# Unused bytes at the ends of two SBUF pools: a diffusion block with hi/lo matmuls, before and after

## The chip, the core and the metric

The kernel runs on one NeuronCore of a Trainium2 chip. Five engines share an on-chip memory, SBUF, of 128 partitions: TensorE (PE in the rows; PEld is its loading of stationary operands), VectorE (DVE), ScalarE (ACT), GpSimd (POOL) and SyncE (SP), which here issues nearly all DMAs. The metric is the device time of one execution in microseconds.

## The reference, cut to what matters

One layer of a diffusion block over 1024 latent tokens of width 1024, with 256 context tokens that are needed only for the end states of a recurrence:

```python
h_c = modulate(rms_norm(ctx, norm1_w), csh1, csc1)
parts_c = split(h_c @ w_in[:, :4096])               # q, forget fwd, forget bwd, i
o_c, s_f, s_b = hgrn_bidir(*parts_c, ..., zero_state, zero_state)
h_x = modulate(rms_norm(x, norm1_w), sh1, sc1)
parts_x = split(h_x @ w_in)                         # 9 parts of 1024 columns
o_x, _, _ = hgrn_bidir(*parts_x[:4], ..., s_f, s_b)
y_a = sgu(gelu(u), gelu(v), ...)                    # spatial gating unit
y_b = hgrn_readout(o_x, og, hgrn_norm_w)
y = (sigmoid(gate_a) * (y_a @ w_a) + sigmoid(gate_b) * (y_b @ w_b)) @ w_o
x = x + g1 * y
h2 = modulate(rms_norm(x, norm2_w), sh2, sc2)
a, v = split(h2 @ w_up)                             # 2 x 2816 columns
x = x + g2 * ((gelu(dwconv_grid(a)) * v) @ w_down)
return rms_norm(x, final_norm_w)
```

## The kernel before, in words

All float32 products of large matrices are made of three matmuls. `mm3` (lines 83 to 89) takes two operands that are each split into a rounded part and a rest, of type float32r, and adds hi x hi (line 87), hi x lo (88) and lo x hi (89) into one PSUM bank; a bank holds 512 float32 and has the tag `pj` or `hg`. In a row `pj<-hxh,whi` the first name behind the arrow is the moving operand (256 or 512 columns) and the second the stationary one (128 columns, loaded anew for every matmul). `load_unit` fetches 512 KB of weights into `wraw` (three buffers), ScalarE makes `whi` of it (line 68), GpSimd or VectorE makes `wlo` (line 69).

The stages follow each other in the program: modulation vectors and context (to about 135 us), eight HGRN heads (to about 880), the gating unit with the `u` projection, gates and branches (880 to 1330), the output projection (to 1426), the ConvFFN's up projection with its convolution on VectorE (lines 1014 and 1016, to 1923), and the down projection (to the end). In most stages the activations move 512 columns at a time against stationary weights: `hxh`/`hxl` in the projections, `yah`/`yal` and `ybh`/`ybl` in the branches, `h2h`/`h2l` in the up projection. In the down projection it is the other way: 512 columns of `w_down` move, and a 128-token slice of `hh`/`hl` (a split hidden tile) is stationary. `hid_split` puts the hidden tiles 0 and 1 and, of each half's tail, the first two (`hs0p if i < 2 else dn`) into the pool `hs0p`; in the second half the tail tiles of the first half come first and are used again. So of 44 uses of a hidden tile (22 tiles, two halves) 8 are from `hs0p` and 36 from `dn`; a use is 8 token blocks x 3 matmuls. In the rows `hh` and `hl` stand for both pools.

The order of all work is the order of the code, with some writes of `tc.issue_after` for ScalarE and VectorE; nothing in it depends on addresses. Pools named "left" (`const`, `wp`, `h1`, `s0p`, `m1`, `ff`, `hs0p`) are stacked up from the low end of SBUF, those named "right" (`hc`, `tmp0`, `ctp`, `hp`, `r1`, `r2`, `sp`, `gp`, `h2`, `bcp`, `cv`, `dn`) down from the high end, and each tile takes its bytes per partition, rounded up to 32. So an address follows from the sizes of the pools that lie below (or above) it. These are the starts, in bytes within a partition; for a pool of several tiles the first:

| Buffers | Use on TensorE | Start before | mod 128 before | Start after | mod 128 after |
|---|---|---|---|---|---|
| `whi` / `wlo` | stationary; moving in the token-major projections, the context's `i`, output and down projections | 17280 / 29568 | 0 | +128 | 0 |
| `hxh`, `mh` | moving, or stationary against 256 columns | 41856 | 0 | 41984 | 0 |
| `hh`, `hl` in `hs0p` | stationary, 512 columns | 131968 | 0 | 132096 | 0 |
| `hh`, `hl` in `dn` | stationary, 512 columns | 184224 | 32 | 183744 | 64 |
| `h2h` / `h2l` | moving, 512 columns | 163808 / 196576 | 96 | 163328 / 196096 | 0 |
| `yah`, `ybh` / `yal`, `ybl` | moving, 512 columns | 131040 / 163808 | 96 | 130560 / 163328 | 0 |
| `hch` / `hcl` | moving or stationary, 256 columns | 212960 / 221152 | 96 | 212480 / 220672 | 0 |
| HGRN tiles `dm`, `e2`, `qb`, `ka`, `v`, `S`, `b` | both, plain float32, 128 columns or fewer | 118432 (`dm`) | 32 | 117952 | 64 |
| HGRN tiles `kt`, `asum`, `osb`; `vt` | stationary, plain float32 | 218976 (`kt`) | 96 | 218496 | 0 |
| `wst`; `vc` | moving, plain float32 | 116224; 116864 | 0 | 115744; 116384 | 32 |
| `apad0` / `apad1` | none (VectorE reads them) | 154272 / 159040 | 32 / 64 | 153792 / 158560 | 64 / 96 |

Slices that a matmul takes of these tiles lie whole multiples of 512 bytes behind the start.

Of the kernel before, what the change touches and what calls it, by code (L numbers as in the profile page):

```python
# [8 lines left out]
F32 = mybir.dt.float32  # L9
# [4 lines left out]
PSUM = bass.MemoryType.PSUM  # L14
DRAM = bass.MemoryType.DRAM

P = 128
# [18 lines left out]
def kernel(  # L36
# [16 lines left out]

    # ------------------------------------------------------------------ pools
    const, close_const = pool("const", "left")
# [16 lines left out]
    def load_unit(src, k0, nk, c0, ncol, lo_eng=None):  # L72
        """weights src[k0*128:(k0+nk)*128, c0:c0+ncol] as two float32r parts [p, k, col]"""
        raw = wp.tile([P, 1024], F32, tag="wraw", name="wraw", bufs=W_RAW)
        last_load[0] = nc.sync.dma_start(
            out=raw.rearrange("p (k n) -> p k n", n=ncol),
            in_=src[k0 * P:(k0 + nk) * P, c0:c0 + ncol].rearrange("(k p) n -> p k n", p=P),
        )
        hi, lo = split_unit(raw, lo_eng)
        v = lambda t: t.rearrange("p (k n) -> p k n", n=ncol)  # L80
        return v(hi), v(lo)

    def mm3(ps, a, b, first, last):
        """ps += a.T @ b for two-part operands a, b"""
        ah, al = a
        bh, bl = b
        nc.tensor.matmul(ps, lhsT=ah, rhs=bh, start=first, stop=False)  # L87
        nc.tensor.matmul(ps, lhsT=ah, rhs=bl, start=False, stop=False)  # L88
        nc.tensor.matmul(ps, lhsT=al, rhs=bh, start=False, stop=last)  # L89

    # -------------------------------------------------------------- constants
    ident = const.tile([P, P], F32, name="ident")
    make_identity(nc, ident)
    ones = const.tile([P, P], F32, name="ones")
# [4 lines left out]
    nc.vector.memset(scanm, 1.0)  # L99
    nc.vector.memset(scanm.rearrange("p (c t) -> p c t", t=CH)[:, :, 0:1], 0.0)  # L100
    hc, close_hc = pool("hc", "right")
    tmp0, close_tmp0 = pool("tmp0", "right")
    trif = tmp0.tile([P, P], F32, name="trif")
    # causal in the direction of the scan, scores transposed [s, t]: two blocks, two directions
    mask = const.tile([P, 2, 2, P], U8, name="mask")
    for d in range(2):
        nc.gpsimd.affine_select(
            out=trif, in_=ones, pattern=[[1 if d == 0 else -1, P]], base=0,
            channel_multiplier=-1 if d == 0 else 1, compare_op=ALU.is_ge, fill=0.0)
        for i in range(2):  # L110
            nc.vector.tensor_copy(out=mask[:, i, d, :], in_=trif)

    ins_of = lambda r: getattr(r, "ins", r)

    def rsqrt(dst, src, n):
        nc.gpsimd.tensor_tensor(out=dst, in0=src, in1=mhalf[:, :n], op=ALU.pow)

    # PSUM: banks of 512 float32
    psp, close_psp = pool("psp", space=PSUM)
# [6 lines left out]

    # ---------------------------------------------------- parameters as columns
    rows = {}
# [28 lines left out]

    # lower bounds: softmax over the depth axis (length one), its cumulative sum less the first row
    lb = const.tile([P, 16], F32, name="lb")
# [13 lines left out]

    # -------------------------------------- modulation: shift1, scale1 (both streams)
    def norm_pair(xt, after):
        """the two row blocks xt[:, i, :] over their rms"""
        ss = const.tile([P, 2], F32, tag="ss", name="ss", bufs=2)
        rs = const.tile([P, 2], F32, tag="rs", name="rs", bufs=2)
        for i in range(2):
            junk = tmp0.tile([P, D], F32, tag="junk", name="junk", bufs=1)  # L180
            with tc.issue_after(after):
                nc.scalar.activation(out=junk, in_=xt[:, i, :], func=AF.Square, accum_out=ss[:, i:i + 1])
        with tc.issue_after(after):
            nc.vector.tensor_scalar(out=ss, in0=ss, scalar1=1.0 / D, scalar2=RMS_EPS, op0=ALU.mult, op1=ALU.add)
        rsqrt(rs, ss, 2)
        for i in range(2):
            with tc.issue_after(after):
                nc.vector.tensor_scalar(out=xt[:, i, :], in0=xt[:, i, :], scalar1=rs[:, i:i + 1], scalar2=None,
                                        op0=ALU.mult)

    ring = lambda: tmp0.tile([P, 2, D], F32, tag="ring", name="ring", bufs=4)
    ctp, close_ctp = pool("ctp", "right")
    # by the tensor engine; of columns 1536..2047 the vector engine sums the first row blocks
    sel = const.tile([P, 2, 2], F32, name="sel")
# [73 lines left out]

    # ------------------------------------------------------ context: final states
    WI = w_in[0]  # L270
# [27 lines left out]
    def first_half(t, d):  # L298
        """the half of each 128-block that comes first in direction d; t [p, blk, 2, 64]"""
        return t[:, :, d, :]  # L300
# [83 lines left out]

    # latent stream
    hxh = [h1.tile([P, T], F32R, name=f"hxh{k}") for k in range(KC)]
# [59 lines left out]

    # --------------------------------------------------------- latent: HGRN2 heads
    hp, close_hp = pool("hp", "right")
# [5 lines left out]

    # the first tags lie where the spatial gating unit starts, the last ones where the context ends
    lead = {}
# [17 lines left out]
    def firsts(t, off, step, nchunk):  # L474
        """[p, d, chunk, t]: of direction d (at off + d * step) the half of each chunk that d meets first"""
        a = t[:]
        return bass.AP(tensor=a.tensor, offset=a.offset + off,
                       ap=[list(a.ap[0]), [step + CH // 2, 2], [CH, nchunk], [1, CH // 2]])
# [3 lines left out]
    def project(off, h, dst_fn, lo_eng=None):  # L482
        """feature-major projection of 128 columns; dst_fn(seg, psum)"""
        wh, wl = load_unit(WI, 0, KC, off + h * P, P, lo_eng)
        for s in range(2):
            ps = pj()
            for k in range(KC):
                mm3(ps, (wh[:, k, :], wl[:, k, :]),
                    (hxh[k][:, s * 512:(s + 1) * 512], hxl[k][:, s * 512:(s + 1) * 512]), k == 0, k == KC - 1)
            dst_fn(s, ps)  # L490

    def token_major(units, n2):
        """token-major projection of two blocks, 256 columns"""
        ps = pj()
        for j in range(2):
            n = 2 * n2 + j
            for k in range(KC):
                wh, wl = units[k // 4]
                mm3(ps[:, j * 256:(j + 1) * 256],
                    (hxh[k][:, n * P:(n + 1) * P], hxl[k][:, n * P:(n + 1) * P]),  # L500
                    (wh[:, k % 4, :], wl[:, k % 4, :]), k == 0, k == KC - 1)
        return ps
# [18 lines left out]
    def finish(h, og, osbs):  # L521
        """read-out of a head, features on partitions, gated; to DRAM"""
        for s in range(2):
# [9 lines left out]
    for h in range(NH):  # L533
# [40 lines left out]
        def state(d, n):  # L574
            """state that block n of direction d starts from"""
            if (d == 0 and n == 0) or (d == 1 and n == NT - 1):
                return s0[:, h, d, :]
            return S[:, d, n, :]

        for st in range(2):  # L580
# [24 lines left out]
            for d in range(2):  # L605
# [17 lines left out]
                                        in1=elv[:, d, :, (1 - d):(2 - d)].to_broadcast([P, 4, CH]), op=ALU.mult)  # L623
            # scores, transposed: [s, t]; pairs with s after and t before the reference are never formed
            nc.scalar.copy(out=firsts(e2z, 0, 0, 8), in_=firsts(e2, 0, 512, 8))
# [63 lines left out]

    # ----------------------------------------------- spatial gating unit (branch A)  # L690
    r1, close_r1 = pool("r1", "right")
# [7 lines left out]
    for q in range(2):  # L699
# [3 lines left out]
        nc.vector.tensor_copy(out=wst[:, 4 * q:4 * q + 4, :].rearrange("p g t -> p (g t)"), in_=tp)  # L703
    # C[d, g, t] = ln_b[d] * sum_s w[g, t, s] + b[g, t]
    for q in range(2):
# [62 lines left out]

    # ---------------------------------------------------------- branches, merged
    gp, close_gp = pool("gp", "right")  # L770
    # modulation rows gate1, shift2, scale2, gate2 (latent): a step is 128 rows of ada_w
    mod_acc = {}
# [86 lines left out]

    # --------------------------------------------- output projection, residual, norm 2  # L860
    close_gp()
# [13 lines left out]
    bcast_row(b2b, mod_d[3])  # L875
    # the residual input, then the updated stream times its norm-2 gain
    xa = [bcp.tile([P, D], F32, name=f"xa{n}") for n in range(NT)]
# [78 lines left out]

    # ------------------------------------------------------------------- ConvFFN
    ff, close_ff = pool("ff", "left")
# [66 lines left out]

    # -------------------------------------------------- down projection, final norm
    dn, close_dn = pool("dn", "right")
# [10 lines left out]
    for half in range(2):  # L1038
# [18 lines left out]
        for n in range(NT):  # L1057
# [10 lines left out]
            else:  # L1068
# [9 lines left out]
                nc.sync.dma_start(out=out[0, n * P:(n + 1) * P, 512:1024], in_=xl)  # L1078
    close_dn()
    close_hs0()  # L1080
    close_ff()
# [34 lines left out]
```

## Time and profile before

| | us |
|---|---|
| Device time, median of 3 runs | 2186.53 (2186.29 to 2187.84) |
| Span of the profiled execution (first to last instruction) | 2181.3 |
| Device time less span | 5.2 |
| TensorE busy in the span | 2138.2 |
| VectorE busy | 1126.6 |
| ScalarE busy | 700.7 |
| GpSimd busy | 446.4 |

The profiled execution's own device time is not listed; the 5.2 us lie outside of its first and last instruction, taken from the median. Busy time of TensorE includes overlap: a 512-column matmul is listed with some 0.39 us, while the next one starts 0.23 us after it. So the time that a matmul costs is read from the distance of two starts in the timeline, not from its listed duration.

### The profile page before, as it was taken

Reading aid. Unit: us, or ns where it says so; the run is one execution under the profiler, and the core shown is the slowest. Engines: PE = TensorE matmul, PEld = TensorE weight load, DVE = VectorE, ACT = ScalarE, POOL = GpSimd, SP = SyncE. Lnnn points to the kernel's source line nnn. Section 1 sums busy time; section 2 is a strip of 40 time slices with the busy share of each in tenths; the row PEclk is TensorE's granted clock in tenths of the full one; section 3 lists DMA queues with packets and bytes.
Section 4 is the critical chain, followed back from the end, with each engine's and each line's share of the span. In section 5 each row is a group of like instructions: output and inputs, shape, how many; then the busy total and the mean of one; then the engine's idle time right before and its main releaser. Section 6 shows DMA issues by size and latency. Waiting matters only on the chain.

```text
span 2181.3 us, 27242 instructions
## 1 busy us (share of the span) xinstructions
PE 2138.2 (98%) x11446; PEld 1795.1 (82%) x11446; DVE 1126.6 (52%) x1513; ACT 700.7 (32%) x999; POOL 446.4 (20%) x243
## 2 busy tenths in 40 slices
PE   8889999999999999999999999999999999999998
PEld 4878889889888899888787788988888888878786
DVE  5784374365356443442214225577677676752424
ACT  3755355345444422221112112232121212132223
POOL 2131122121221202122122211322121222121110
PEclk9989999999999999999999999999999999999999
DMA  6620111111111111113335235212111111121212
GB/s 262 204 87 29 40 40 59 30 39 49 43 36 40 49 49 54 44 58 107 97 95 175 69 107 178 86 49 58 39 49 49 48 49 39 39 97 49 87 39 97
DMA packets 183579, 158.72 MB, mean 73 GB/s; under 512 B 5459, under 2 KB 163480, under 8 KB 182433
## 3 DMA queue, kind: packets, MB, share of 16 engines
q1 hardware_dynamic: 182289, 154.89, 22.8%
q8 instruction: 90, 1.47, 0.3%
q10 hardware_dynamic: 1168, 2.10, 0.3%
q14 instruction: 32, 0.26, 0.0%
HBM read 144.37 MB, written 12.60 MB: 72 GB/s over the span
## 4 chain that ended last, share of the span: by engine, by line
PE 83%; DVE 8%; issue 3%; DMA 2%; ACT 2%; POOL 0%; SPq 0%; POOLq 0%; ACTq 0%; DVEq 0%
PE pj L87 17%; PE pj L89 17%; PE pj L88 17%; PE hg L87 8%; PE hg L89 8%; PE hg L88 8%; PE hg L651 1%; PE hg L633 1%; DMA wraw<-in_w_in_dram 1%; PE hg L670 1%; PE hg L757 1%; PE hg L639 1%; DVE b L314 1%; DVE wlo L69 1%; DVE b L316 1%
## 5 line engine op out<-in xcount | busy, mean ns | idle before, releaser
L69 POOL TENSOR_TENSOR wlo<-wraw,whi 128x1024 fp32r<-128x1024 f32 x146 | 363.1, 2490 | 1248.4 <-ACT whi L68 1220.5
L68 ACT CAST whi<-wraw 128x1024 fp32r<-128x1024 f32 x186 | 194.7, 1050 | 564.8 <-PE pj L88 283.7
L87 PE MATMUL pj<-hxh,whi 128*128 128x512 f32 x896 | 353.5, 395 | 0.2 <-ACT hxh L398 0.2
L88 PE MATMUL pj<-hxl,whi 128*128 128x512 f32 x896 | 351.4, 392 | 1.0 <-POOL hxl L399 1.0
L89 PE MATMUL pj<-hxh,wlo 128*128 128x512 f32 x896 | 351.4, 392 | 0.0
L1016 DVE SCALAR_TENSOR_TENSOR hid<-apad,cw,hid 128x1024 f32<-128x1024 f32 x176 | 271.8, 1545 | 6.3
L87 PEld LDWEIGHTS pj<-hxh,whi 128*128 128x128 f32 x896 | 168.7, 188 | 35.8 <-ACT whi L68 1.7
L89 PEld LDWEIGHTS pj<-hxh,wlo 128*128 128x128 f32 x896 | 168.7, 188 | 34.3
L88 PEld LDWEIGHTS pj<-hxl,whi 128*128 128x128 f32 x896 | 168.6, 188 | 34.3 <-POOL hxl L399 1.4
L87 PE MATMUL pj<-whi,hxh 128*128 128x256 f32 x512 | 145.4, 285 | 0.0
L88 PE MATMUL pj<-wlo,hxh 128*128 128x256 f32 x512 | 145.2, 284 | 0.0
L89 PE MATMUL pj<-whi,hxl 128*128 128x256 f32 x512 | 145.0, 283 | 0.0
L87 PE MATMUL pj<-h2h,whi 128*128 128x512 f32 x352 | 140.6, 400 | 0.0
L87 PE MATMUL hg<-h2h,whi 128*128 128x512 f32 x352 | 140.6, 399 | 0.0
L89 PE MATMUL pj<-h2h,wlo 128*128 128x512 f32 x352 | 138.8, 394 | 0.0
L89 PE MATMUL hg<-h2h,wlo 128*128 128x512 f32 x352 | 138.7, 394 | 0.0
L88 PE MATMUL hg<-h2l,whi 128*128 128x512 f32 x352 | 138.1, 392 | 0.0
L88 PE MATMUL pj<-h2l,whi 128*128 128x512 f32 x352 | 138.1, 392 | 0.0
L314 DVE TENSOR_TENSOR_SCAN b<-scanm,g 128x512 f32<-128x512 bf16 (+1 forms) x24 | 26.1, 1087 | 177.0 <-ACT g L561 174.7
L745 DVE TENSOR_TENSOR hl<-hid,hh 128x1024 fp32r<-128x1024 f32 x38 | 48.3, 1283 | 120.1 <-ACT hh L744 120.1
L1014 DVE TENSOR_SCALAR hid<-apad,cw 128x1024 f32<-128x1024 f32 x22 | 55.3, 2512 | 95.8 <-ACT apad L1000 95.8
L785 DVE SCALAR_TENSOR_TENSOR acc<-maw,sc,acc 128x1024 f32<-128x1024 f32 x32 | 43.1, 1347 | 115.2 <-DMA maw<-in_ada_w_dram 112.5
(276 smaller groups left out, 4317.4 us busy)
## 6 DMA issues: line engine op xcount, KB each, us to landing
wraw<-in_w_in_dram SPq DMA_DIRECT2D x96, 512.0 KB
wraw<-in_ffn_w_up_dram SPq DMA_DIRECT2D x44, 512.0 KB
maw<-in_ada_w_dram SPq DMA_DIRECT2D x32, 512.0 KB
wraw<-in_ffn_w_down_dram SPq DMA_DIRECT2D x22, 512.0 KB
ring<-in_ada_w_dram SPq DMA_DIRECT2D x8, 1024.0 KB
ring<-in_x_dram SPq DMA_DIRECT2D x4, 1024.0 KB
yb_d<-og SPq DMA_DIRECT2D x8, 512.0 KB
wraw<-in_w_branch_a_dram SPq DMA_DIRECT2D x8, 512.0 KB
```

The lines of the kernel that those rows point to most:

```text
L68: nc.scalar.copy(out=hi, in_=raw)
L69: (lo_eng or nc.gpsimd).tensor_tensor(out=lo, in0=raw, in1=hi.bitcast(F32), op=ALU.subtract)
L87: nc.tensor.matmul(ps, lhsT=ah, rhs=bh, start=first, stop=False)
L88: nc.tensor.matmul(ps, lhsT=ah, rhs=bl, start=False, stop=False)
L89: nc.tensor.matmul(ps, lhsT=al, rhs=bh, start=False, stop=last)
L314: nc.vector.tensor_tensor_scan(out=b, data0=scanm[:, :n], data1=g, initial=0.0, op0=ALU.mult, op1=ALU.add)
L316: nc.vector.tensor_tensor_scan(out=b[:, ::-1], data0=scanm[:, :n], data1=g[:, ::-1], initial=0.0, op0=ALU.mult, op1=ALU.add)
L633: nc.tensor.matmul(quart(spv[:, i, d, :])[:, :, 1 - d, :], lhsT=e2[:, d, blk], rhs=quart(dm[:, d, blk])[:, :, 1 - d, :], start=True, stop= ...
L745: (lo_eng or nc.vector).tensor_tensor(out=lo, in0=src, in1=hi.bitcast(F32), op=ALU.subtract)
L785: nc.vector.scalar_tensor_tensor(out=acc, in0=aw, scalar=sc[:, k, 0:1], in1=acc, op0=ALU.mult, op1=ALU.add)
L1014: nc.vector.tensor_scalar(out=acc, in0=src, scalar1=w_, scalar2=None, op0=ALU.mult)
L1016: nc.vector.scalar_tensor_tensor(out=acc, in0=src, scalar=w_, in1=acc, op0=ALU.mult, op1=ALU.add)
```

## The change

Two tiles are allocated that nothing reads or writes: 128 bytes per partition at the end of `const`, ahead of all other pools of the left side, and 480 bytes in a new pool `padr`, which is the first on the right side and is closed last. All left pools behind `const` (and the tiles of `const` that are allocated later than this line) move up by 128 bytes, all right pools move down by 480. Nothing else differs but comments, which are left out here:

```diff
+    padr, close_padr = pool("padr", "right")
+    padr.tile([P, 120], F32, name="padr")
     hc, close_hc = pool("hc", "right")
     tmp0, close_tmp0 = pool("tmp0", "right")
     trif = tmp0.tile([P, P], F32, name="trif")
...
+    const.tile([P, 32], F32, name="cpad")
+
     ins_of = lambda r: getattr(r, "ins", r)
...
     close_dn()
+    close_padr()
     close_hs0()
```

The instructions of every engine, their order, and the semaphores that they wait for and raise are the same in both programs; only addresses differ.

## Rows read from the trace of the kernel before

**Rows 1.** The page: span, then busy time, share and instructions of each engine.

```profile
span 2181.3 us, 27242 instructions
...
PE 2138.2 (98%) x11446; PEld 1795.1 (82%) x11446; DVE 1126.6 (52%) x1513; ACT 700.7 (32%) x999; POOL 446.4 (20%) x243
```

**Rows 2.** The page: the chain that ended last, by line.

```profile
PE pj L87 17%; PE pj L89 17%; PE pj L88 17%; PE hg L87 8%; PE hg L89 8%; PE hg L88 8%; PE hg L651 1%; PE hg L633 1%; DMA wraw<-in_w_in_dram 1%; PE hg L670 1%; PE hg L757 1%; PE hg L639 1%; DVE b L314 1%; DVE wlo L69 1%; DVE b L316 1%
```

**Rows 3.** Windows: us; busy PE, PEld, DVE, ACT, POOL; PEclk; DMA; GB/s.

```profile
1450.00:1900.00 450.00, 450.00 (x1931) 362.10 (x1930) 330.21 (x224) 90.12 (x103) 97.55 (x41) 1.00 0.16 46
...
1950.00:2150.00 200.00, 199.43 (x857) 160.51 (x856) 66.95 (x66) 53.89 (x66) 30.90 (x13) 1.00 0.16 51
```

**Rows 4.** Groups of instructions by line and form; count, busy us, mean ns.

```profile
L87 PE MATMUL pj<-hxh,whi 128*128 128x512 f32 x896 | 353.5, 395 | 0.2 <-ACT hxh L398 0.2
...
L87 PE MATMUL pj<-h2h,whi 128*128 128x512 f32 x352 | 140.6, 400 | 0.0
...
L87 PE MATMUL pj<-whi,hh 128*128 128x512 f32 x176 | 69.6, 395 | 2.3 <-ACT hh L744 2.3
...
L87 PE MATMUL hg<-yah,whi 128*128 128x512 f32 x128 | 50.3, 393 | 0.0
...
L651 PE MATMUL hg<-v,kt 128*128 128x128 f32 x256 | 35.7, 282 | 1.3 <-ACT kt L647 1.2
```

**Rows 5.** Timeline of PE, gate A then branch A: start us, listed us.

```profile
1036.42 0.39 PE L87 MATMUL pj<-hxh,whi 128*128 128x512 f32 x1
...
1044.35 0.39 PE L89 MATMUL pj<-hxh,wlo 128*128 128x512 f32 x1
...
1047.86 0.40 PE L89 MATMUL hg<-yah,wlo 128*128 128x512 f32 x1
...
1055.56 0.40 PE L89 MATMUL hg<-yah,wlo 128*128 128x512 f32 x1
```

**Rows 6.** Timeline of PE, up projection.

```profile
1499.79 0.40 PE L87 MATMUL pj<-h2h,whi 128*128 128x512 f32 x1
...
1507.49 0.40 PE L87 MATMUL hg<-h2h,whi 128*128 128x512 f32 x1
```

**Rows 7.** Timeline of PE, down projection: hidden tiles 0 and 1, then 2.

```profile
1924.68 0.39 PE L87 MATMUL pj<-whi,hh 128*128 128x512 f32 x1
...
1933.52 0.39 PE L87 MATMUL hg<-whi,hh 128*128 128x512 f32 x1
...
1940.63 0.40 PE L87 MATMUL pj<-whi,hh 128*128 128x512 f32 x1
...
1944.83 0.40 PE L87 MATMUL pj<-whi,hh 128*128 128x512 f32 x1
```

**Rows 8.** Timeline of PE, 256 columns: context `i`, context gates, output projection.

```profile
49.67 0.28 PE L87 MATMUL pj<-whi,hch 128*128 128x256 f32 x1
...
52.49 0.28 PE L87 MATMUL pj<-whi,hch 128*128 128x256 f32 x1
...
96.14 0.28 PE L87 MATMUL pj<-hch,whi 128*128 128x256 f32 x1
...
101.18 0.28 PE L87 MATMUL pj<-hch,whi 128*128 128x256 f32 x1
...
1334.74 0.28 PE L87 MATMUL pj<-whi,mh 128*128 128x256 f32 x1
...
1337.98 0.28 PE L87 MATMUL pj<-whi,mh 128*128 128x256 f32 x1
```

**Rows 9.** Timeline of DVE, two hidden tiles of the up projection.

```profile
1784.87 2.51 DVE L1014 TENSOR_SCALAR hid<-apad,cw 128x1024 f32<-128x1024 f32 x1 [4.64 <-ACT apad L1000]
...
1787.41 12.71 DVE L1016 SCALAR_TENSOR_TENSOR hid<-apad,cw,hid 128x1024 f32<-128x1024 f32 x8
...
1807.27 2.51 DVE L1014 TENSOR_SCALAR hid<-apad,cw 128x1024 f32<-128x1024 f32 x1 [4.64 <-ACT apad L1000]
...
1809.81 12.71 DVE L1016 SCALAR_TENSOR_TENSOR hid<-apad,cw,hid 128x1024 f32<-128x1024 f32 x8
```

## Prediction

> **What bounds the kernel.** I read the page first: TensorE is busy for 2138.2 of the 2181.3 us of the span [rows 1], and six of the lines in the chain that ended last are the three lines of `mm3` on the two kinds of PSUM bank, with 17% for each on `pj` [rows 2]. [...] So what a matmul costs is the distance to the start of the next, and the timeline gives it. This is where the change has to show.
>
> The instructions, their order and their waits stay, so only the speed of single instructions can change, and the question is whether the trace already shows one kind of instruction at both kinds of address. It does.
>
> - Gate A moves 512 columns of `hxh` (start a multiple of 128) against `whi`: from 1036.42 to 1044.35 us there are 35 steps, 226.6 ns each. Right behind it branch A moves 512 columns of `yah` (96 beyond a multiple of 128) against the same weights buffers: from 1047.86 to 1055.56 there are 33 steps, 233.3 ns each [rows 5].
> - The up projection moves `h2h` (96 beyond): 33 steps from 1499.79 to 1507.49, 233.3 ns. Here the steps go through both kinds of bank, `pj` and `hg`, so the bank is not the reason [rows 6].
> - The down projection has the aligned weights as the moving side. With hidden tiles 0 and 1 (from `hs0p`, a multiple of 128) as stationary side there are 39 steps from 1924.68 to 1933.52, 226.7 ns; with tile 2 (from `dn`, 32 beyond) 18 steps from 1940.63 to 1944.83, 233.3 ns [rows 7]. Same lines, same banks, same moving buffers, some 10 us apart; what differs between the tiles is their place.
>
> So a 512-column matmul takes 6.7 ns more when either operand starts at an odd multiple of 32. [...]
>
> **The change part by part.** The 480 bytes on the right side first; they carry the gain.
>
> 1. Up projection. The row `pj<-h2h,whi` counts 352 [rows 4]; there are six like it (three lines, two banks), 2112 matmuls. From 96 beyond to a multiple of 128, like `hxh`: 2112 x 6.7 ns = 14.2 us.
> 2. Branches. `hg<-yah,whi` counts 128 [rows 4]; six like it with `ybh`, 768 matmuls: 768 x 6.7 ns = 5.1 us.
> 3. Down projection. `pj<-whi,hh` counts 176 [rows 4]; six like it, 1056 matmuls in 44 uses of 24. 36 uses are of tiles in `dn`: 864 matmuls, 864 x 6.7 ns = 5.8 us. These tiles come to 64 beyond a multiple of 128, a remainder that no 512-column operand of the trace has. So the term lies between 0 and 5.8 us. I take 5.8, because the only remainders known to be slow, 32 and 96, are the odd multiples of 32, but keep 0 for the range and as a rival.
> 4. Context, 256 columns. As moving operand `hch` (96 beyond) takes 42 steps from 96.14 to 101.18, 120.0 ns; as stationary operand 24 steps from 49.67 to 52.49, 117.5 ns. The aligned `mh` as stationary operand takes 27 steps from 1334.74 to 1337.98, 120.0 ns [rows 8]. So with 256 columns alignment gains nothing, and for the 192 matmuls of the context's `i` projection it may lose 2.5 ns each: 0.5 us. I count the loss.
> 5. HGRN and gating unit, plain float32 with 128 columns or fewer. Seven kinds of row from 112 to 256 records, the largest being `hg<-v,kt` with 256 [rows 4], together some 1250, change from 32 beyond to 64 beyond on one or both sides (`kt` and `asum` to 0). The trace shows no such matmul with both operands aligned. Bounds from the nearest rows: a gain of 6.7 ns each as with 512 columns, 8.4 us, or a loss of 2.5 ns each as in the context, 3.1 us. They are short, and so nearest to the 256-column rows, where the effect is between nothing and the small loss: I take 0 and keep both ends. `wst` and `vc` become misaligned as moving operands of some 190 records; with 6.7 ns that is 1.3 us at most, and I take 0 for the same reason.
> 6. The other engines. Tiles such as `xa`, `ut`, `bsb` and `x3` get starts at odd multiples of 32, and others leave them. VectorE shows what that does: `apad0` starts at an odd, `apad1` at an even multiple of 32, and successive hidden tiles use them in turn, with 2.51 and 12.71 us both times [rows 9]. Cost nothing. If it did cost, TensorE would hide it: in the up projection VectorE sits idle for 4.64 us of each 22.40 us period.
>
> The 128 bytes on the left side move operands that are multiples of 128 to other multiples of 128. I take 0 for them; whether that holds is the rival that ends on the other side.
>
> Does the gain arrive at the end? In the up projection the period of a hidden tile is 96 matmuls, 22.40 us; it becomes 96 x 226.7 ns = 21.76 us, and VectorE's idle 4.64 us become 4.0. GpSimd needs 98 of 450 us, ScalarE 90 [rows 3]. So TensorE stays the bound and the gain goes through whole. Ahead of tile 2 in the down projection there is a wait (15 steps from 1933.52 to 1940.63 us, 3.7 us more than their speed asks for [rows 7]): the first split into `dn` is made late. It moves along unchanged.
>
> Sum: 14.2 + 5.1 + 5.8 - 0.5 = 24.6 us. The span would go from 2181.3 to 2156.7 us; with the 5.2 us outside the span unchanged, the median from 2186.5 to **2162 us**.
>
> [...]
>
> [...]
>
> **The rivals.**
>
> - *Multiples of 64 are not enough.* `dn`'s tiles, at 64 beyond a multiple of 128, stay at 233.3 ns. For it: all fast operands that the trace has are multiples of 128. Against it: nothing direct. Time: 2162 + 5.8 = 2168 us. Chance 0.13.
> - *More than forecast.* The short float32 matmuls gain as the long ones do, 8.4 us: 2153 us. For it: they too change from an odd multiple of 32. Against it: the 256-column rows, with no gain [rows 8]. Chance 0.10.
> - *No change.* The start of an operand has no price, and the two speeds belong to something else in these stages that the padding leaves alone: 2186.5 us. [...] Against it: three pairs of rows with the same answer [rows 5 to 7]. Chance 0.05.
> - *Slower.* All operands that are fast before (`whi`, `wlo`, `hxh`, `hs0p`) start not at any multiple of 128, but at 384 beyond a multiple of 512; the left padding takes them to a multiple of 512. If position within 512 is what counts, and a multiple of 512 is no good one, the 2688 `hxh` matmuls (three rows of 896 [rows 4]) and the 192 of `hs0p` go to 233.3 ns, and the right side stays there: 2880 x 6.7 ns = 19.3 us, 2206 us. With the right side's gain kept, it ends slower from 24.6 us / 2880 = 8.5 ns per matmul on. Against it: slices of 512 bytes and halves of 2048 bytes are used in turn with an even 226.6 ns, so the distance between the operands doesn't matter in such steps. Chance 0.04.
>
> **How the numbers follow.** The forecast has the remaining 0.68, and 2162 us. Around it the unknown costs are 8.4 us of gain (to 2153) and 3.1 + 1.3 us of loss (to 2166); the first rival with a part of that loss reaches 2171. The range 2152 to 2171 takes these in and leaves out the last two rivals, with 0.09. This kernel's runs lie within 0.07% of each other, so 0.2% (4.4 us) is about what a measurement can tell from no change. Faster by more than that: the forecast and the first two rivals, 0.68 + 0.13 + 0.10 = 0.91. Within 0.2%: 0.05. Slower: 0.04.
>
> **What the profile after would show.** Starts of `yah` and `h2h` matmuls 226.7 ns apart; the listed mean of `pj<-h2h,whi` down from 400 to about the 395 of `hxh` [rows 4]; the period of a hidden tile 21.76 us with VectorE's operations at 2.51 and 12.71 us [rows 9]; `hh` tiles 2 onward at 226.7 ns (233.3 by the first rival); `hxh` unchanged at 226.6 (233.3 by the last). The prediction is wrong if a step in the up projection stays at 233.3, or if TensorE begins to wait there, in the column of idle time, for `whi`, `wlo` or a PSUM bank.

## The result, and the profile after

The changed kernel takes 2161.07 us (median of 4 runs, 2160.8 to 2164.55) against 2186.6 us (4 runs, 2186.29 to 2187.84): a ratio of 0.988 (0.987 to 0.990). The forecast was 2162 us. Medians here and below are of the fast executions of a kernel; the few slower ones (one of 25 of the kernel before, for example) are left out. The time and the stages came out nearly as forecast. The reason that the prediction gave did not hold: the experiments below show it.

The page of the profile after: span, then busy time, share and instructions of each engine [rows 1].

```profile
span 2159.0 us, 27242 instructions
...
PE 2114.8 (98%) x11446; PEld 1794.1 (83%) x11446; DVE 1122.9 (52%) x1513; ACT 701.0 (32%) x999; POOL 447.0 (21%) x243
```

The span is 22.3 us shorter and TensorE is busy for 23.4 us less; the other engines stay within 4 us. The timeline of PE after (start us, listed us), for the stages of [rows 5 to 8]: 256 columns (here of `hxh`), branch A, up projection, then `hh` tile 2 of the down projection.

```profile
859.77 0.28 PE L87 MATMUL pj<-whi,hxh 128*128 128x256 f32 x1
...
860.85 0.28 PE L87 MATMUL pj<-whi,hxh 128*128 128x256 f32 x1
...
1043.16 0.39 PE L87 MATMUL hg<-yah,whi 128*128 128x512 f32 x1
...
1053.36 0.39 PE L87 MATMUL hg<-yah,whi 128*128 128x512 f32 x1
...
1500.16 0.39 PE L87 MATMUL hg<-h2h,whi 128*128 128x512 f32 x1
...
1507.64 0.39 PE L87 MATMUL hg<-h2h,whi 128*128 128x512 f32 x1
...
1916.80 0.50 PE L87 MATMUL pj<-whi,hh 128*128 128x512 f32 x1 [2.35 <-ACT hh L748]
...
1918.92 0.63 PE L87 MATMUL hg<-whi,hh 128*128 128x512 f32 x1
...
1920.63 0.63 PE L88 MATMUL pj<-wlo,hh 128*128 128x512 f32 x1
...
1923.45 0.39 PE L87 MATMUL pj<-whi,hh 128*128 128x512 f32 x1
...
1929.63 0.39 PE L87 MATMUL hg<-whi,hh 128*128 128x512 f32 x1
```

`yah`: 45 steps in 10.20 us, 226.7 ns. `h2h`: 33 steps in 7.48 us, 226.7 ns. Both were 233.3. `hh` in `dn`: 27 steps in 6.18 us, 228.9 ns: neither the 233.3 of before nor the 226.7 of the forecast. The 256 columns stay at 120.0 ns (9 steps in 1.08 us). The groups of lines with their mean duration, as in [rows 4]:

```profile
L87 PE MATMUL pj<-hxh,whi 128*128 128x512 f32 x896 | 353.0, 394 | 0.2 <-ACT hxh L402 0.2
...
L87 PE MATMUL pj<-h2h,whi 128*128 128x512 f32 x352 | 137.0, 390 | 0.0
...
L655 PE MATMUL hg<-v,kt 128*128 128x128 f32 x256 | 35.6, 282 | 1.4 <-ACT kt L651 1.3
```

`h2h` goes from 400 to 390 ns, even below `hxh`; the plain float32 row stays at 282. VectorE in the up projection, as in [rows 9]:

```profile
1790.75 2.50 DVE L1018 TENSOR_SCALAR hid<-apad,cw 128x1024 f32<-128x1024 f32 x1 [4.17 <-ACT apad L1004]
1793.29 12.54 DVE L1020 SCALAR_TENSOR_TENSOR hid<-apad,cw,hid 128x1024 f32<-128x1024 f32 x8
...
1812.51 2.50 DVE L1018 TENSOR_SCALAR hid<-apad,cw 128x1024 f32<-128x1024 f32 x1 [4.17 <-ACT apad L1004]
```

The period is 21.76 us as forecast, VectorE's idle time 4.17 us. The windows after (PE busy is the second number, PEclk the third from the end) show that TensorE still has no gap in the up projection, and the clock in a short stretch of the down projection:

```profile
1450.00:1900.00 450.00, 450.00 (x1987) 372.59 (x1986) 332.06 (x231) 93.81 (x108) 97.20 (x42) 1.00 0.16 47
...
1916.00:1922.00 6.00, 4.41 (x12) 3.26 (x13) 6.00 (x7) 5.48 (x6) 1.39 (x1) 0.72 0.95 337
```

Behind the wait for `hh` in front of tile 2 (2.35 us) the granted clock is 0.72 in the mean over 6 us: between 1918.92 and 1920.63 us four steps take 427 ns each, where the steps from 1923.45 us on take 228.9. Some seven such steps cost 1.4 us. The trace of before had the same wait of 2.3 us with no such stretch (clock 1.00 on both sides of it). The stretch does not hang on the gain: all ten other traces of whole kernels have it at this place, with 7 to 13 slow steps, those of the kernels below that gained nothing too. Only the traced execution of before ran without it; no other execution of that kernel was traced.

By the first matmul of each stage, the spans changed by: HGRN heads -0.2 us (from the first matmul on `hxh` to the first of the gating unit, on `wsraw`, at 798 us), gating unit -0.3, branches A and B -2.9 and -2.8, output projection 0.0, up projection -13.9, down projection -2.4.

### The profile page after: what moved, and what is told of

The parts are those of the page before. It is cut to its first block, busy times and chain, and to the rows that moved or that the text cites. A ratio compares the mean times of both kernels' runs of the same rounds, so it can differ in the third digit from the quotient of the medians.

```text
span 2159.0 us, 27242 instructions
## 1 busy us (share of the span) xinstructions
PE 2114.8 (98%) x11446; PEld 1794.1 (83%) x11446; DVE 1122.9 (52%) x1513; ACT 701.0 (32%) x999; POOL 447.0 (21%) x243
## 4 chain that ended last, share of the span: by engine, by line
PE 82%; DVE 8%; issue 3%; ACT 3%; DMA 2%; POOL 0%; SPq 0%; POOLq 0%; ACTq 0%; DVEq 0%
PE pj L89 17%; PE pj L88 17%; PE pj L87 17%; PE hg L88 8%; PE hg L87 8%; PE hg L89 8%; PE hg L655 1%; PE hg L637 1%; PE pj L238 1%; PE hg L674 1%; PE hg L761 1%; DVE b L318 1%; PE hg L643 1%; DMA ring<-in_ada_w_dram 1%; DVE b L320 1%
```

## The experiments

Two theories. *Own remainder*, the prediction's: a matmul is slow when one of its operands starts at an odd multiple of 32 bytes. *Distance*: what counts is the start of the moving operand less that of the stationary one, modulo 256; 0 is fast. In the kernel before, `whi`, `hxh`, `mh` and `hs0p` all start at 128 modulo 256, so `hxh` is at distance 0, `h2h` and `yah` at 96, `dn`'s tiles at 224: the rows of before cannot tell the two apart.

### One side alone, and other sizes of the right side

Each edit is against the changed kernel. First the left padding is taken out, then the right one, then the right one is made 448 or 416 bytes.

```diff
-    const.tile([P, 32], F32, name="cpad")          # e1_right_only

-    padr, close_padr = pool("padr", "right")       # e2_left_only
-    padr.tile([P, 120], F32, name="padr")
...
-    close_padr()

-    padr.tile([P, 120], F32, name="padr")
+    padr.tile([P, 112], F32, name="padr")          # e3_right_448
+    padr.tile([P, 104], F32, name="padr")          # e4_right_416
```

> Only the 480 bytes on the right side; the left pools stand as before. Theory (the remainder of a 512-column matmul's operand start by 128 sets its price): all of the gain is here, 0.988 of before, 2161 us; h2h and yah steps 226.7 ns, hh of dn 228.9 ns. Rival (the left side's move to multiples of 512 carries a part): less than that, in the limit no gain, 2186 us.

> Only the 128 bytes on the left side; every right pool keeps its odd multiple of 32. Theory: no change within 0.1%, 2186 us, h2h steps 233.3 ns. Rival (left side carries a part): 2 to 25 us faster.

> Both pads, the right one 448 bytes in place of 480: nearly the same shift, but every right operand is at another odd multiple of 32 (yah, h2h from 96 to 32 beyond a multiple of 128, hh of dn from 32 to 96). Theory: as before, 2186 us within 2 us, all three at 233.3 ns a step. Rival (any shift breaks an unlucky pairing of places, or only one of the remainders 32 and 96 is slow): faster by 5 to 25 us.

> Both pads, the right one 416 bytes: yah, h2h start 64 beyond a multiple of 128, hh of dn and the HGRN tiles dm, e2, v, S, b at a multiple of 128. Theory: hh of dn 226.7 ns a step (5.8 us less than before). For h2h and yah the theory leaves open what 64 costs as moving side: at 228.9 ns as the stationary hh has it after the change, 2186.5 - 5.8 - 2880 x 4.4 ns = 2168 us; at 226.7 ns 2161 us; at 233.3 ns 2181 us. HGRN stage unchanged within 1 us; if aligned short float32 matmuls are cheaper, up to 8 us less there.

Against the kernel before, measured beside them (2185.97 us): right alone 2186.21 us, ratio 0.9998 (0.9989 to 1.0008); left alone 2183.53, 0.9987 (0.9978 to 0.9997); 448 bytes 2185.42, 0.9998 (0.9988 to 1.0007); 416 bytes 2168.99, 0.9918 (0.9900 to 0.9935). The timeline of PE of the kernel with the right side alone, up projection:

```profile
1599.72 0.39 PE L87 MATMUL hg<-h2h,whi 128*128 128x512 f32 x1
...
1603.89 0.40 PE L87 MATMUL pj<-h2h,whi 128*128 128x512 f32 x1
```

18 steps in 4.17 us, 231.7 ns (232.4 over the stage), although `h2h` now starts at a multiple of 512 and `whi` at a multiple of 128. Own remainder asks for 226.7 here and has fallen. By distance it is 0 - 384, that is 128 modulo 256. With 448 bytes `h2h`, `yah` and `dn` are at distance 32 and take 233.3 to 233.6 ns, as both theories ask. With 416 bytes `dn`'s tiles are at distance 0 and take 226.7 ns, and `h2h` stands at 64 from `whi`; its timeline:

```profile
1599.81 0.39 PE L87 MATMUL pj<-h2h,whi 128*128 128x512 f32 x1
...
1603.93 0.39 PE L87 MATMUL hg<-h2h,whi 128*128 128x512 f32 x1
```

18 steps in 4.12 us, 228.9 ns. Left alone has a ratio just under 1, with `h2h`, `yah` and `dn` still at 233.3 or 233.4; where its 2.5 us come from was not found.

The run with 416 bytes answers another question. It puts `dm`, `e2`, `v`, `S` and `b` of the HGRN heads at multiples of 128, and the heads take 664.0 us against 663.1 before: the short plain float32 matmuls gain nothing that shows there.

### The same steps with nothing at a multiple of 64

The right padding is taken out, and the left one is 96 bytes. Then `whi`, `hxh`, `yah` and `h2h` all start at 224 modulo 256, an odd multiple of 32, at distance 0 from each other.

```diff
-    padr, close_padr = pool("padr", "right")
-    padr.tile([P, 120], F32, name="padr")
...
-    const.tile([P, 32], F32, name="cpad")
+    const.tile([P, 24], F32, name="cpad")
...
-    close_padr()
```

> No bytes on the right side; 96 on the left in place of 128. whi, wlo, hxh, hh of hs0p now start 96 beyond a multiple of 128, as yah and h2h did before and still do: not one of these operands is at a multiple of 64, and moving and stationary start are equal by 256. Theory 2: hxh stays at 226.7 ns, yah and h2h go to 226.7, hh of dn (moving 64 past the stationary start by 256) to 228.9 as in the changed kernel: 2186 - 19.3 - 3.8 = 2163 us. Theory 1 (multiples of 64 or 128): all of them at 233.3, hxh too, 2186 + 19 = 2205 us.

2161.97 us (2158.74 to 2163.31) against 2186.72: 0.9885 (0.9861 to 0.9908), the gain of the change itself. The timeline of PE, up projection:

```profile
1599.95 0.39 PE L87 MATMUL pj<-h2h,whi 128*128 128x512 f32 x1
...
1604.03 0.39 PE L87 MATMUL pj<-h2h,whi 128*128 128x512 f32 x1
```

18 steps in 4.08 us, 226.7 ns. This decides it for the kernel: with 512 columns the steps took 226.7 ns with no operand at a multiple of 64, the two sides standing at the same place modulo 256.

### Matmuls alone

Two programs leave out the reference's computation and run only matmuls, 96 of each pair of operands, over four PSUM banks, with chosen starts. The first pairs starts in steps of 32 bytes (and a few of 4 and 16) and has three types; the second goes through the distance in steps of 16 bytes, with the moving operand at 0 (`rma`) and at 128 (`rmb`), the stationary one at 16 times its letter's place (`rsa` 0, `rsb` 16, ...); `q` in a name is the same with 256 columns.

```python
for i in range(96):
    nc.tensor.matmul(bank, lhsT=stationary[...], rhs=moving[...], start=..., stop=...)
```

> Leaves out the whole computation of the reference: only matmuls on a part of x, 96 in a row of each kind, with moving and stationary operand at chosen starts (a 0, b 32, c 64, d 96, e 16, f 4, g 48 bytes past a multiple of 128). Theory: float32r with 512 columns 226.7 ns a step with both at 0, 233.3 with either at 32 or 96, 228.9 with the stationary at 64; the starts 4, 16 and 48 as slow as 32. Rival (what counts is the distance between the two operands): bb, cc and dd as fast as aa. [...] 256 columns: aa 120.0, moving at 32 120.0, stationary at 32 or 96 117.5. float32 with 128 columns: no difference above 1 ns.

> Leaves out the whole computation of the reference: float32r matmuls, 96 in a row of each kind, 512 columns (names r) and 256 (names q), moving start 0 (a) or 128 (b) past a multiple of 512, stationary start 16 bytes further with each letter (a 0, b 16, ... p 240). Theory 2 (what counts is how far apart the two starts lie, by 256): 512 columns 226.7 ns a step for ra,sa and rb,si alone (distance 0) and 228.9 for ra,sm (the stationary 64 bytes short of the moving start, 192 past it by 256), the rest 231 to 240. Theory 1 (each operand's own remainder by 128): ra and rb alike, 226.7 with stationary a and i, slower elsewhere. 256 columns: 120.0 at distance 0; other distances between 113 and 120, as the first table of starts had it.

The timeline of PE of the first program (start of each group of 96; what a group takes is the distance to the next start). Starts modulo 512: `rsa` 128, `rmb` 288 and `rsb` 32, `rmc` 448 and `rsc` 192, `rmd` 96 and `rsd` 352, `rme` 144; `f` is plain float32, with 192 records for 96 matmuls, `h` bfloat16.

```profile
53.99 22.56 PE L63 MATMUL bank<-rmc,rsa 128*128 128x512 f32 x96
76.39 22.56 PE L63 MATMUL bank<-rmd,rsa 128*128 128x512 f32 x96
98.79 22.40 PE L63 MATMUL bank<-rme,rsa 128*128 128x512 f32 x96
121.03 23.19 PE L63 MATMUL bank<-rmf,rsa 128*128 128x512 f32 x96
...
278.03 21.94 PE L63 MATMUL bank<-rmb,rsb 128*128 128x512 f32 x96
299.81 22.56 PE L63 MATMUL bank<-rmb,rsc 128*128 128x512 f32 x96
322.21 22.66 PE L63 MATMUL bank<-rmc,rsb 128*128 128x512 f32 x96
344.70 21.94 PE L63 MATMUL bank<-rmc,rsc 128*128 128x512 f32 x96
366.48 21.96 PE L63 MATMUL bank<-rmd,rsd 128*128 128x512 f32 x96
...
543.82 21.65 PE L63 MATMUL bank<-fma,fsa 128*128 128x128 f32 x192
565.30 21.60 PE L63 MATMUL bank<-fmb,fsa 128*128 128x128 f32 x192
586.74 21.60 PE L63 MATMUL bank<-fma,fsb 128*128 128x128 f32 x192
...
629.62 20.88 PE L63 MATMUL bank<-hma,hsa 128*128 128x512 bf16 x96
650.34 20.88 PE L63 MATMUL bank<-hmb,hsa 128*128 128x512 bf16 x96
```

`rmb,rsb`, both at odd multiples of 32 and 256 apart: 21.78 us, 226.9 ns. `rmb,rsc`, 96 apart: 22.40 us, 233.3 ns. `rmc,rsc`, 256 apart: 226.9 ns again. The first pair of this program, `rma` and `rsa`, stands at multiples of 128 and 128 apart; behind its first dozen slow steps it settles at 232.4 ns, where own remainder asked for 226.7. Plain float32 (21.48 and 21.44 us, distances 96 to 160) and bfloat16 (20.72 us, 215.8 ns, distances 0 to 224) take the same at all starts that were tried. The second program:

```profile
31.12 21.93 PE L58 MATMUL bank<-rma,rsb 128*128 128x512 f32 x96
52.89 22.55 PE L58 MATMUL bank<-rma,rsc 128*128 128x512 f32 x96
75.28 22.56 PE L58 MATMUL bank<-rma,rsd 128*128 128x512 f32 x96
...
276.49 22.14 PE L58 MATMUL bank<-rma,rsm 128*128 128x512 f32 x96
298.47 22.56 PE L58 MATMUL bank<-rma,rsn 128*128 128x512 f32 x96
...
454.22 21.93 PE L58 MATMUL bank<-rmb,rsi 128*128 128x512 f32 x96
475.99 22.55 PE L58 MATMUL bank<-rmb,rsk 128*128 128x512 f32 x96
...
588.80 11.05 PE L58 MATMUL bank<-qma,qse 128*128 128x256 f32 x96
599.68 11.57 PE L58 MATMUL bank<-qma,qsf 128*128 128x256 f32 x96
...
793.20 11.47 PE L58 MATMUL bank<-qmb,qsm 128*128 128x256 f32 x96
804.51 11.43 PE L58 MATMUL bank<-qmb,qso 128*128 128x256 f32 x96
```

From the first start to the next: 16 bytes apart (`rma,rsb`) 21.77 us, 226.8 ns; 32 apart (`rma,rsc`) 22.39 us, 233.2 ns; moving 64 past stationary (`rma,rsm`) 21.98 us, 229.0 ns; distance 0 with both at 128 (`rmb,rsi`) 226.8 ns. In this program, with 512 columns, 0 and 16 to either side are the fast distances, 64 is 2.2 ns slower, 80 (229.9) and 176 (231.9) lie between, 160 is at 234.2, and all the others at 233.2 to 233.4; with the moving operand at 128, where only multiples of 32 were tried, the values are the same. With 256 columns distance 0 is not the best: 120.0 ns, while 192 gives 113.3 with the moving operand at 0 (`qma,qse`, 10.88 us) and 117.8 with it at 128 (`qmb,qsm`, 11.31 us).

Three things do not fit a price that hangs on the distance alone. In the first program `rmc,rsa`, moving 64 past stationary, took 22.40 us, 233.3 and not 228.9 ns, and `rme,rsa`, moving 16 past it, 22.24 us, 231.7 and not 226.8. Distance 128 takes 232.4 ns there and in the kernel with the right side alone, and 233.3 in the second program. Why was not found. Distance 0 was fast in every pair of both programs, 226.7 to 227.1 ns once the first slow steps were past.

### The down projection's tiles

`dn`'s tiles are moved down by 64 bytes (to a multiple of 128, at distance 128) or by 192 bytes (distance 0); beside them the changed kernel once more.

```diff
+    dn.tile([P, 16], F32, name="dpad")             # e5_dn_128
+    dn.tile([P, 48], F32, name="dpad")             # e8_dn_192
```

> The changed kernel with 64 more unused bytes at the end of the pool dn, so that hh and hl of dn start at a multiple of 128 in place of 64 beyond one. Theory (a stationary operand at 64 costs a third of what it costs at 32): their steps go from 228.9 to 226.7 ns, 864 x 2.2 ns = 1.9 us less than the changed kernel, 2159 us. Rival (multiples of 64 are as good as multiples of 128, and 228.9 ns has another cause, such as the pairing with the moving side): the steps stay at 228.9 ns, no change.

> The changed kernel again, beside the version with the aligned dn on the same chip: 2161 us, for the comparison.

> The changed kernel with 192 more unused bytes in dn in place of 64, so that hh and hl of dn start at a multiple of 256, as the weights that move against them do. Theory 2: their steps go from 228.9 to 226.7 ns, 864 x 2.2 ns = 1.9 us less than the changed kernel. Theory 1: no better than with 64 bytes (232.4 ns a step, 4 us more than the changed kernel), since both are multiples of 128.

At multiples of 128: 2167.20 us, 0.9916 (0.9903 to 0.9930), against 2163.21, 0.9896 (0.9882 to 0.9910), for the changed kernel beside it. So better alignment of these tiles costs some 4 us, where the expectation had a gain of 1.9 us and its rival no change; in the traces the down projection takes 250.9 us, first to last matmul, against 247.5 after. The timelines of PE, kernel with 64 bytes, then with 192 bytes:

```profile
1974.65 0.39 PE L87 MATMUL hg<-whi,hh 128*128 128x512 f32 x1
...
1980.23 0.40 PE L87 MATMUL hg<-whi,hh 128*128 128x512 f32 x1
```

```profile
1974.71 0.39 PE L87 MATMUL hg<-whi,hh 128*128 128x512 f32 x1
...
1980.15 0.39 PE L87 MATMUL hg<-whi,hh 128*128 128x512 f32 x1
```

24 steps each: 5.58 us, 232.5 ns, and 5.44 us, 226.7 ns. With 192 bytes the down projection takes 245.9 us against 247.5 after: 1.6 us less, where 864 x 2.2 ns = 1.9 us are due. In the time (2162.81 us, 0.9889 with 0.9866 to 0.9911) that is too little to be seen between runs that lie 3 to 5 us apart.

### A better place for 256 columns too

The 96 bytes on the left and the 192 bytes in `dn` together, and for the projections with 256 columns `whi` and `wlo` are taken 192 bytes further on in slots that are 256 bytes longer (`trif` shares a slot to make room).

```diff
-        hi = wp.tile([P, 1024], F32R, tag="whi", name="whi", bufs=W_SPL)
+        hi = wp.tile([P, 1088], F32R, tag="whi", name="whi", bufs=W_SPL)[:, past:past + 1024]
...
-        hi, lo = split_unit(raw, lo_eng)
+        hi, lo = split_unit(raw, lo_eng, 48 if ncol == 256 else 0)
...
-    trif = tmp0.tile([P, P], F32, name="trif")
+    trif = tmp0.tile([P, D], F32, tag="junk", name="trif", bufs=1)[:, 0:P]
```

> As e7_left_96, with three more edits: 192 unused bytes in dn (its hh and hl at distance 0 from the weights by 256); whi and wlo lie 4352 bytes apart, and units of 256 columns (the moving side of the token-major projections, the context's i and the output projection) lie 192 bytes further in their tiles, so that the moving start is 192 past the stationary one by 256; trif is the first part of the tile junk, to make room. Theory 2: 512 columns all at 226.7 ns; 256 columns leave 120.0 for 113.3 ns (seen at this distance in two of four runs of the small kernels) or 117.8 (the other two): 2304 steps of hxh and mh x 6.7 or 2.2 ns, so 15.4 or 5.1 us, and 1.9 us in dn, below the changed kernel's 2161 to 2163 us: 2145 or 2155 us. Theory 1: no gain from a distance; 2161 us or more.

2153.66 us (2152.52 to 2155.1) against 2186.11: 0.985 (0.9835 to 0.9868), faster than both kernels. The timeline of PE at the place shown above for the kernel after:

```profile
859.81 0.28 PE L88 MATMUL pj<-wlo,hxh 128*128 128x256 f32 x1
...
861.62 0.28 PE L89 MATMUL pj<-whi,hxl 128*128 128x256 f32 x1
```

16 steps in 1.81 us, 113.1 ns against 120.0. Not all bursts are like it: some run at 117.8 ns, and in this trace a burst keeps from its first few steps on to its end what it has. The mean is 115.9 ns on `hxh` (1536 matmuls) and 116.6 on `mh` (768): 1536 x 4.1 + 768 x 3.4 ns = 8.9 us. The stages became 6.3 us shorter by it, not 8.9: heads and gating unit take 838.2 us against 843.0 with the 96 bytes alone, the output projection 96.3 against 97.7, though these stages differ by 1 us and more between other traces. The forecasts of 2145 and 2155 us took one rhythm each; the kernel has both. (At this distance stand three groups of the small programs, not four: two at 113.3 ns and one at 117.8.)

## Why the prediction came out

- **Sizes.** Up projection: forecast 14.2 us, measured 13.9. Branches: 5.1, measured 5.7. Both rest on 226.7 and 233.3 ns, which held to 0.1 ns, and TensorE stayed the bound (busy for 450.00 of 450 us), so the gain went through whole. The two speeds were read rightly; that the change would bring the fast one rested on a wrong rule, and that it did was luck.
- **The step that failed** is "a 512-column matmul takes 6.7 ns more when either operand starts at an odd multiple of 32". The kernel with 96 bytes has every operand of the up projection and the branches at an odd multiple of 32 and takes 226.7 ns there; the one with the right side alone has them all at multiples of 128 and takes 232.4 in the up projection. What the runs show in its place is the distance of the two starts modulo 256: 226.7 ns at 0, 233.3 at the 96 of before.
- **The left padding** was taken at 0, and the 480 bytes were to "carry the gain". By themselves they bring nothing that the runs can tell (ratio 0.9998, 0.9989 to 1.0008). Neither side carries the gain: with 128 on the left and 480 on the right the weights on one side and `yah`, `ybh`, `h2h` on the other all come to 0 modulo 256. The number was right only because the forecast was made for both together.
- **Distance was dropped too early.** The prediction wrote that "the distance between the operands doesn't matter in such steps". It had seen slices 512 and 2048 bytes apart; both are multiples of 256, and so the rows said nothing on other distances. The rival that ended slower (a multiple of 512 as a bad place) rested on position as well, and nothing of it was seen.
- **Third term mis-sized.** Forecast 5.8 us, measured 2.4 between the two traces. The tiles stand 64 from `whi`, where a step takes 228.9 ns: 864 x 4.4 = 3.8 us. The other 1.4 us are the stretch at the lower clock (0.72 over 6 us) behind the wait for `hh`, which of all traces only that of before lacks. The rival "Multiples of 64 are not enough" asked for 233.3 ns and 2168 us, which did not come; and at a multiple of 128 these tiles are slower than at 64 (232.4 ns).
- **Terms at or near 0.** HGRN and gating unit: -0.2 us in the heads, and no gain with 416 bytes either: right. Context: `hch` as stationary operand went from 117.6 to 119.9 ns as forecast, 0.4 us, which doesn't stand out of the few us by which the first stages differ between executions. VectorE's operations: 2.50 and 12.54 us, as before or a little shorter.
- **The frame.** The 5.2 us "outside the span" mixed two executions: in each later run the device time lies 1.8 us above its own span (2160.8 and 2159.0), so the profiled execution of before was some 3 us faster than its median. Its mean granted clock was 0.995; the executions of before that gave the 2185.97 us have 0.991 to 0.995, mostly 0.993, as the kernel after has. The medians differ by 25.5 us, the spans by 22.3; the sum of 24.6 lies between by luck as much as by its terms.

Open is what makes the distance count. Either side can be moved (the stationary operand alone by 16 bytes: from 226.8 to 233.2 ns), and in bfloat16 all starts that were tried took 215.8 ns. No run holds one stationary operand over several matmuls, which would tell whether a fresh one for every matmul is needed for the effect.

## What to carry to other kernels

Where float32r matmuls with a fresh stationary operand bound a stage, read the step from start to start for each pair of buffers, and set the steps against the difference of the two starts modulo 256, not against either start alone; with 512 columns make it 0 (226.7 ns here, against 233.3 at 96); in this kernel 96 unused bytes at one place did what the change does with 608 at two. Before a rule is read out of a few addresses, list which other quantity goes through the same values in these rows: here one operand was always at 128 modulo 256, so remainder and distance could not be told apart. When two edits come together, forecast each alone as well. And before a small difference between two traces is put down to the change, see whether the granted clock fell at the same places in both (here 1.00 before and 0.72 after behind the wait for `hh`).

## What the runs showed of the hardware that was not expected

- The best distance is not the same for both widths: 0 (and 16 to either side) for 512 columns, 192 for 256 columns (113.3 or 117.8 against 120.0 ns).
- With 256 columns at 192 there are two steady rhythms, 113.3 and 117.8 ns, and a burst keeps the one that it settles on. What selects it is open. Whether such rhythms are also behind the pairs with 512 columns that did not fit was not tried.
- After the same wait of 2.3 to 2.4 us in the down projection some matmuls took 427 against some 230 ns a step in ten of eleven traces: seven or eight steps in six of them, 12 or 13 in those of right alone, left alone, 448 and 416 bytes. Only the trace of before has none. What decides it was not tried. In the traces whose clock is shown it fell there: 0.72 over 6 us in that of after, 0.76 over 7 us in that of the kernel with 64 bytes in `dn`, PEclk third from the end:

```profile
1919.00:1926.00 7.00, 5.56 (x16) 4.14 (x17) 7.00 (x7) 5.33 (x6) 2.55 (x1) 0.76 0.77 283
```

- A moving operand that starts 4 bytes beyond a multiple of 128 (`rmf,rsa`, 96 steps in 23.03 us) took 239.9 ns, slower than any distance in multiples of 16 (at most 234.3 ns in the two small programs, the first group of each left out, which begins with slow steps).
